# Gate one-hots in pairs of tokens, a U tile in every second gate step, and gate sums evicted with four tokens innermost

## The chip, the cores and the metric

The kernel runs on one core of a Trainium2 chip. The metric is the device time of one execution in microseconds (us). Before the change the median of 3 runs is 2675.46 us, from 2675.15 to 2679.0. The engines of the core are TensorE (matmuls, PE in the profile; its weight loads are PEld), VectorE (DVE), ScalarE (ACT), GpSimd (POOL) and SyncE (SP), whose queue issues most of the DMA transfers.

## The reference, cut to what matters

The program is two transformer blocks over 512 tokens of width 1024. The change lies in the PEER layer at the end of the first block. For every token, 8 heads choose 16 experts each out of 128 x 128, by the best sums of two keys, and a softmax over the 16 gives the gates. An expert is one row of `expert_u` and one of `expert_v`:

```python
eidx = take_along_axis(cand_idx, pos)      # i * 128 + j, for 512 tokens x 8 heads x 16
g = softmax(best)
for each block of tokens:
    u = expert_u[ib]                       # ib, gb: eidx and g of the block
    a = gelu(einsum('thkd,td->thk', u, xb))
    w = gb * a
    out = einsum('thk,thkd->td', w, expert_v[ib])
```

## The kernel before

The first three blocks of 128 tokens (`TD` = 384 tokens) do not gather rows of experts. They multiply all 16384 experts: `u_tile` makes Gelu(U h) for 128 experts and 384 tokens, `weighted` multiplies that with the gate sums of these experts, and `add_rows` multiplies the product with 128 rows of `expert_v` and adds it up in PSUM. The fourth block gathers its rows by indirect DMA (lines 938 to 957), spread over the same main loop of 128 steps (lines 1018 to 1039).

Gate sums are what `peer_gates` makes from line 1191 on. For one token, the 128 choices (8 heads x 16) lie on the partitions. A one-hot matrix `oj` says which second key j each choice has, and `o1` and `o2` say which first key i, times the gate in two fp16 parts. Two matmuls of 128x128x128 (lines 1229 and 1230) give the sum of gates for each (j, i) of that token. There are 384 tokens, so 768 such matmuls. A one-hot of 128 is the product of a high digit of 8 and a low digit of 16 (`onehot`, line 1219, on VectorE), and the digits themselves are compared with a ramp `rt` for 96 tokens at a time (`digit`, line 1202). The work goes in 48 steps of 8 tokens: three one-hots, two PSUM tiles `g_gp` of four tokens each, and two evictions by ScalarE (line 1232) to `g_sg`. Four steps fill a `g_sg` of 32 tokens, which goes to DRAM (`b_gd`, 2 MB, line 1235). The main loop reads it back as `b_g`, four experts' rows of keys at a time (line 965), and needs all 12 parts for its first step.

In DRAM and in `g_sg` the order is key i, then token. In the one-hots four tokens lie innermost: `[groups of 4 tokens, 128 keys, 4 tokens]`, so the columns of one token are 4 elements apart. The one-hot tiles have two buffers each, `g_gp` has four and `g_sg` two.

A U tile needs 512 KB of U by the SP queue, a split into a high and a low part (`w_hi` on ScalarE, `w_lo` on VectorE, lines 71 and 72), 24 matmuls of 128x384 (lines 76 to 78, `b_ups`) and a Gelu on ScalarE (line 915). U tiles do not depend on the gates, so they are strewn over `peer_gates` to fill TensorE: 28 calls stand ahead of the gate steps, 16 in them (every third step) and 2 after them (line 920). The activated tiles 0 to 9 lie in a part of `x` that is free for that time (`NX` = 10), the others in a pool of `NAB` = 36, and `b_ups` has two PSUM banks. A place of the pool is free again when `weighted` (line 969) has read it, and from step 10 on the main loop calls `u_tile` once in each step. The order on each engine is made by a scheduler that keeps the program's order as a priority, and lets an instruction pass another that is not ready.

Of the kernel before, what the change touches and what calls it, by code (L numbers as in the profile page):

```python
# [13 lines left out]
FP16 = mybir.dt.float16  # L14
I32 = mybir.dt.int32
U32 = mybir.dt.uint32
AF = mybir.ActivationFunctionType
OP = mybir.AluOpType
# [829 lines left out]
GS = 32768.0  # L848
# [4 lines left out]
GT = 32  # L853
OG = 8
DG = 3
# [27 lines left out]
def phase_b(K):  # L883
    nc, tc, d = K.nc, K.tc, K.d
    V, S, PE = nc.vector, nc.scalar, nc.tensor
    with ExitStack() as st:
# [31 lines left out]
        with ExitStack() as s1:  # L918
            peer_gates(K, s1, P, hT, small, gd, eg, gg3, u_tile)
# [132 lines left out]
def peer_gates(K, st, P, hT, small, gd, eg, gg3, u_tile):  # L1052
    nc, tc, d = K.nc, K.tc, K.d
    V, S, PE = nc.vector, nc.scalar, nc.tensor
    tk = st.enter_context(tc.tile_pool(name="g_tk", bufs=1))
    tT = tk.tile([128, 6, TD], FP16, name="g_tT")
    rt = tk.tile([128, 16, 16], FP16, name="g_rt")
    with ExitStack() as s0:
# [4 lines left out]
        with ExitStack() as s1:  # L1063
# [18 lines left out]
            for hp in range(16):  # L1082
                w, ps = began.pop(0)
# [25 lines left out]
        for b in range(NB):  # L1109
# [3 lines left out]
            for i in range(5):  # L1113
                n = LENS[i]
# [15 lines left out]
        n = NB * 128  # L1130
# [60 lines left out]
    with ExitStack() as s2:  # L1191
        ohp = s2.enter_context(tc.tile_pool(name="g_ohp", bufs=2))
        stg = s2.enter_context(tc.tile_pool(name="g_stg", bufs=2))
        gps = s2.enter_context(tc.tile_pool(name="g_gps", bufs=4, space=PSUM))
        dg = s2.enter_context(tc.tile_pool(name="g_dg", bufs=1))
        G4 = DG * GT // 4
        for c in range(TD // GT):
            if c % DG == 0:
                ts = slice(c * GT, (c + DG) * GT)
                token = lambda w: tT[:, w, ts].rearrange("p (g t) -> p g t", t=4)[:, :, None, :]  # L1200

                def digit(w, n):

                    t = dg.tile([128, G4, n, 4], FP16, name=f"g_d{w}")
                    V.tensor_tensor(t[:], token(w).to_broadcast(t[:].shape),
                                    rt[:, None, 0:n, 0:4].to_broadcast(t[:].shape), op=OP.is_equal)
                    return t[:]

                ih, jh, il, jl = digit(0, 8), digit(1, 8), digit(2, 16), digit(3, 16)
                ih0, ih1 = [dg.tile([128, G4, 8, 4], FP16, name=f"g_d{w}")[:] for w in (4, 5)]  # L1210
                for w, t in ((4, ih0), (5, ih1)):
                    V.tensor_tensor(t, ih, token(w).to_broadcast(t.shape), op=OP.mult)
            sg = stg.tile([128, 128, GT], F32, name="g_sg")
            for t8 in range(GT // OG):
                g0 = ((c % DG) * GT + t8 * OG) // 4
                gs = slice(g0, g0 + OG // 4)
                shape = [128, OG // 4, 8, 16, 4]

                def onehot(hi, lo, name):
                    t = ohp.tile([128, OG // 4, 128, 4], FP16, name=name)  # L1220
                    V.tensor_tensor(t[:].rearrange("p g (a b) t -> p g a b t", a=8), hi[:, gs, :, None].to_broadcast(shape),
                                    lo[:, gs, None].to_broadcast(shape), op=OP.mult)
                    return t

                oj, o1, o2 = onehot(jh, jl, "g_oj"), onehot(ih0, il, "g_o1"), onehot(ih1, il, "g_o2")
                for g in range(OG // 4):
                    ps = gps.tile([128, 4, 128], F32, name="g_gp")
                    for t in range(4):
                        PE.matmul(ps[:, t], oj[:, g, :, t], o1[:, g, :, t], start=True, stop=False)  # L1229
                        PE.matmul(ps[:, t], oj[:, g, :, t], o2[:, g, :, t], start=False, stop=True)  # L1230
                    tq = t8 * OG + 4 * g
                    S.activation(sg[:, :, tq:tq + 4].rearrange("p i t -> p t i"), ps[:], AF.Copy, scale=1.0 / GS)
                if (c * (GT // OG) + t8) % 3 == 0:
                    u_tile()
            nc.sync.dma_start(gd[:, :, c].rearrange("q p n -> p q n"), sg[:].rearrange("p (q i) t -> p q (i t)", i=4))

# [1147 lines left out]
```

## Time and profile before

| | |
|---|---|
| median of 3 runs | 2675.46 us |
| the profiled execution | 2677.02 us |
| its span, first to last instruction | 2675.2 us |
| TensorE busy (matmuls) | 2536.6 us, 95% |
| VectorE busy | 1781.9 us, 67% |
| ScalarE busy | 961.8 us, 36% |
| granted clock of TensorE, mean | 0.972 of full speed |
| gate steps, first to last matmul | 590.9 to 748.6 us |
| first matmul of the main loop | 767.25 us |

Shares of the span are means over stages that have different limits. The stage of the gate steps is some 160 us long, and the table says nothing about it alone; views of that stretch do.

### The profile page before, as it was taken

The numbers are of one execution on the slowest core, as the hardware profiler recorded it, in microseconds if no ns is written. First come the engines' busy times: TensorE is split into PE (matmuls) and PEld (weight loads), VectorE is DVE, ScalarE is ACT, GpSimd is POOL, SyncE is SP. The second block draws the span as 40 slices with busy tenths as digits, with TensorE's granted clock in tenths as the row PEclk, the third lists the DMA queues.
The fourth block names the chain that finished last, engine by engine and source line by source line (L and its number), as shares of the span: only waits on it lengthen the run. The fifth ranks groups of instructions, "written<-read, shape, count | busy, mean of one in ns | idle before, by whom it ended". The sixth has DMA issues, their size and how long they took to land.

```text
span 2675.2 us, 43755 instructions
## 1 busy us (share of the span) xinstructions
PE 2536.6 (95%) x17112; PEld 2121.5 (79%) x17112; DVE 1781.9 (67%) x3794; ACT 961.8 (36%) x1603; POOL 390.1 (15%) x269
## 2 busy tenths in 40 slices
PE   5999999899989999999999998999999989999985
PEld 4987888899978999999999887888797856555664
DVE  6654689987757777778878797676753673333334
ACT  3431432457743333333333335343532411111112
POOL 0000000000013455555545320000000000000001
PEclk8999899999999999999999999998999999999988
DMA  6226222236787899989988883222132489998896
GB/s 233 80 93 235 79 81 81 103 126 202 217 285 282 318 325 326 325 323 321 328 325 320 300 302 125 87 80 71 64 116 110 180 336 392 390 395 355 346 415 260
DMA packets 183485, 623.93 MB, mean 233 GB/s; under 512 B 15847, under 2 KB 66407, under 8 KB 156651
## 3 DMA queue, kind: packets, MB, share of 16 engines
q1 hardware_dynamic: 146410, 486.87, 48.6%
q0 software_dynamic: 36864, 134.23, 14.4%
q8 instruction: 135, 2.21, 0.3%
q14 instruction: 76, 0.61, 0.1%
HBM read 591.55 MB, written 29.49 MB: 232 GB/s over the span
## 4 chain that ended last, share of the span: by engine, by line
PE 82%; DVE 10%; DMA 5%; ACT 2%; issue 1%; SPq 0%; DVEq 0%; ACTq 0%
PE f_hp L1889 6%; PE b_acc L77 6%; PE b_acc L78 6%; PE b_acc L76 6%; PE b_ups L78 6%; PE b_ups L76 6%; PE b_ups L77 6%; PE p_acc L76 5%; PE p_acc L77 5%; PE p_acc L78 5%; PE f_yp L1931 3%; DMA f_w<-in_w 3%; PE f_xp L1788 2%; PE g_gp L1229 2%; PE g_gp L1230 2%; DVE w_lo L72 2%
## 5 line engine op out<-in xcount | busy, mean ns | idle before, releaser
L72 DVE TENSOR_TENSOR w_lo<-w_raw,w_hi 128x1024 fp32r<-128x1024 f32 x228 | 277.8, 1219 | 247.1 <-ACT w_hi L71 246.8
L71 ACT CAST w_hi<-w_raw 128x1024 fp32r<-128x1024 f32 x228 | 239.0, 1048 | 548.8 <-PE b_ups L77 281.1
L78 PE MATMUL b_ups<-hT,w_lo 128*128 128x384 f32 x1024 | 347.8, 340 | 6.7 <-DVE w_lo L72 6.5
L76 PE MATMUL b_ups<-hT,w_hi 128*128 128x384 f32 x1024 | 347.7, 340 | 1.3 <-ACT x_sb L915 1.0
L77 PE MATMUL b_ups<-hT,w_hi 128*128 128x384 f32 x1024 | 345.4, 337 | 0.0
L938 POOL DMA_INDIRECT x_sb<-in_u_rows,b_eg x128 | 193.4, 1511 | 991.2 <-ACT w_hi L71 767.8
L77 PE MATMUL b_acc<-b_vl,b_wh 128*128 128x512 f32 x756 | 296.8, 393 | 9.0 <-DVE b_vl L72 9.0
L76 PE MATMUL b_acc<-b_vh,b_wh 128*128 128x512 f32 x756 | 295.1, 391 | 1.7 <-ACT b_vh L71 1.7
L78 PE MATMUL b_acc<-b_vh,b_wl 128*128 128x512 f32 x756 | 296.1, 392 | 0.0
L77 PE MATMUL p_acc<-w_lo,hT 128*128 128x256 f32 x896 | 255.2, 285 | 9.5 <-DVE w_lo L72 9.5
L76 PE MATMUL p_acc<-w_hi,hT 128*128 128x256 f32 x896 | 257.7, 288 | 2.6 <-ACT hT L71 2.0
L78 PE MATMUL p_acc<-w_hi,hT 128*128 128x256 f32 x896 | 254.8, 285 | 0.2 <-DVE hT L72 0.2
L938 POOL DMA_INDIRECT x_sb<-in_v,b_eg x128 | 186.5, 1457 | 219.4 <-DVE b_accg L955 188.4
L78 PEld LDWEIGHTS b_ups<-hT,w_lo 128*128 128x128 f32 x1024 | 194.0, 189 | 8.6 <-DVE w_lo L72 8.6
L76 PEld LDWEIGHTS b_ups<-hT,w_hi 128*128 128x128 f32 x1024 | 194.0, 189 | 5.1 <-ACT x_sb L915 1.3
L77 PEld LDWEIGHTS b_ups<-hT,w_hi 128*128 128x128 f32 x1024 | 193.5, 189 | 3.2
L76 PEld LDWEIGHTS p_acc<-w_hi,hT 128*128 128x128 f32 x896 | 171.9, 192 | 18.6 <-issue 13.2
L77 PEld LDWEIGHTS p_acc<-w_lo,hT 128*128 128x128 f32 x896 | 172.5, 193 | 11.2 <-DVE w_lo L72 10.7
L71 ACT CAST b_wh<-b_wfull 128x384 fp32r<-128x384 f32 x128 | 65.6, 514 | 320.7 <-PE b_acc L77 317.7
L77 PEld LDWEIGHTS b_acc<-b_vl,b_wh 128*128 128x128 f32 x756 | 143.0, 189 | 37.8 <-DVE b_vl L72 10.7
L78 PEld LDWEIGHTS p_acc<-w_hi,hT 128*128 128x128 f32 x896 | 172.2, 192 | 1.0 <-DVE hT L72 0.4
L945 DVE SCALAR_TENSOR_TENSOR b_junkg<-x_sb,h2g 128x1024 bf16<-128x1024 f32 x128 | 156.3, 1221 | 24.9 <-DMA x_sb<-in_u_rows,b_eg 23.3
(659 smaller groups left out, 5083.6 us busy)
## 6 DMA issues: line engine op xcount, KB each, us to landing
f_w<-in_w SPq DMA_DIRECT2D x192, 1024.0 KB
w_raw<-in_u SPq DMA_DIRECT2D x128, 512.0 KB
b_vraw<-in_v SPq DMA_DIRECT2D x128, 512.0 KB
b_gd<-g_sg SPq DMA_DIRECT2D x12, 2048.0 KB
b_g<-b_gd SPq DMA_DIRECT2D x32, 768.0 KB
a_ar_t<-in_w_ada SPq DMA_DIRECT2D x32, 512.0 KB
w_raw<-in_w_tok SPq DMA_DIRECT2D x20, 512.0 KB
a_ar_t<-in_w_ada SPq DMA_DIRECT2D x8, 1024.0 KB
```

What stands on the lines that cost most here:

```text
L71: self.nc.scalar.copy(hi, src)
L72: self.nc.vector.tensor_tensor(lo, src, hi, op=OP.subtract)
L76: first = mm(ps, a[0], b[0], start=start, stop=False)
L77: mm(ps, a[0], b[1], start=False, stop=False)
L78: mm(ps, a[1], b[0], start=False, stop=stop)
L938: nc.gpsimd.indirect_dma_start(out=r, out_offset=None, in_=d[src], in_offset=bass.IndirectOffsetOnAxis(ap=eg[:, k:k + 1], axis=0))
L945: tc.keep_in_program_order(V.scalar_tensor_tensor(junk[:], r, 1.0, h2g[:], op0=OP.mult, op1=OP.mult, accum_out=ag[:, k:k + 1]))
L1229: PE.matmul(ps[:, t], oj[:, g, :, t], o1[:, g, :, t], start=True, stop=False)
L1230: PE.matmul(ps[:, t], oj[:, g, :, t], o2[:, g, :, t], start=False, stop=True)
L1788: PE.matmul(room[k // 4][:, k % 4, :n], hs[i][:, b, k * 128:(k + 1) * 128], sel[:, b, :n], start=k % 4 == 0 and i == 0 and b == 0, stop=i ...
L1889: last = PE.matmul(p, X[:, k], ts["w31", k // 2][:, c0:c0 + 512], start=k == 0, stop=k == 7, skip_group_check=True)
L1931: PE.matmul(p, gT[k], ts["w2", hf][:, k * 512:(k + 1) * 512], start=k == 0, stop=k == 3, skip_group_check=True)
```

## The change

One-hots and digits hold two tokens innermost instead of four, in twice as many groups, so that the columns of one token are 2 elements apart. The number of instructions and their sizes stay. A U tile is called for in every second of the 48 steps (24 calls) instead of every third (16). The eviction still reads the same PSUM tile and writes the same elements of `g_sg`, but goes through them key by key with the four tokens innermost, instead of token by token with the 128 keys innermost.

```diff
@@ -1193,31 +1193,31 @@
         stg = s2.enter_context(tc.tile_pool(name="g_stg", bufs=2))
         gps = s2.enter_context(tc.tile_pool(name="g_gps", bufs=4, space=PSUM))
         dg = s2.enter_context(tc.tile_pool(name="g_dg", bufs=1))
-        G4 = DG * GT // 4
+        GN = DG * GT // 2
         for c in range(TD // GT):
             if c % DG == 0:
                 ts = slice(c * GT, (c + DG) * GT)
-                token = lambda w: tT[:, w, ts].rearrange("p (g t) -> p g t", t=4)[:, :, None, :]
+                token = lambda w: tT[:, w, ts].rearrange("p (g t) -> p g t", t=2)[:, :, None, :]
 
                 def digit(w, n):
 
-                    t = dg.tile([128, G4, n, 4], FP16, name=f"g_d{w}")
+                    t = dg.tile([128, GN, n, 2], FP16, name=f"g_d{w}")
                     V.tensor_tensor(t[:], token(w).to_broadcast(t[:].shape),
-                                    rt[:, None, 0:n, 0:4].to_broadcast(t[:].shape), op=OP.is_equal)
+                                    rt[:, None, 0:n, 0:2].to_broadcast(t[:].shape), op=OP.is_equal)
                     return t[:]
 
                 ih, jh, il, jl = digit(0, 8), digit(1, 8), digit(2, 16), digit(3, 16)
-                ih0, ih1 = [dg.tile([128, G4, 8, 4], FP16, name=f"g_d{w}")[:] for w in (4, 5)]
+                ih0, ih1 = [dg.tile([128, GN, 8, 2], FP16, name=f"g_d{w}")[:] for w in (4, 5)]
                 for w, t in ((4, ih0), (5, ih1)):
                     V.tensor_tensor(t, ih, token(w).to_broadcast(t.shape), op=OP.mult)
             sg = stg.tile([128, 128, GT], F32, name="g_sg")
             for t8 in range(GT // OG):
-                g0 = ((c % DG) * GT + t8 * OG) // 4
-                gs = slice(g0, g0 + OG // 4)
-                shape = [128, OG // 4, 8, 16, 4]
+                g0 = ((c % DG) * GT + t8 * OG) // 2
+                gs = slice(g0, g0 + OG // 2)
+                shape = [128, OG // 2, 8, 16, 2]
 
                 def onehot(hi, lo, name):
-                    t = ohp.tile([128, OG // 4, 128, 4], FP16, name=name)
+                    t = ohp.tile([128, OG // 2, 128, 2], FP16, name=name)
                     V.tensor_tensor(t[:].rearrange("p g (a b) t -> p g a b t", a=8), hi[:, gs, :, None].to_broadcast(shape),
                                     lo[:, gs, None].to_broadcast(shape), op=OP.mult)
                     return t
@@ -1225,12 +1225,13 @@
                 oj, o1, o2 = onehot(jh, jl, "g_oj"), onehot(ih0, il, "g_o1"), onehot(ih1, il, "g_o2")
                 for g in range(OG // 4):
                     ps = gps.tile([128, 4, 128], F32, name="g_gp")
-                    for t in range(4):
-                        PE.matmul(ps[:, t], oj[:, g, :, t], o1[:, g, :, t], start=True, stop=False)
-                        PE.matmul(ps[:, t], oj[:, g, :, t], o2[:, g, :, t], start=False, stop=True)
+                    for q in range(4):
+                        j, t = divmod(4 * g + q, 2)
+                        PE.matmul(ps[:, q], oj[:, j, :, t], o1[:, j, :, t], start=True, stop=False)
+                        PE.matmul(ps[:, q], oj[:, j, :, t], o2[:, j, :, t], start=False, stop=True)
                     tq = t8 * OG + 4 * g
-                    S.activation(sg[:, :, tq:tq + 4].rearrange("p i t -> p t i"), ps[:], AF.Copy, scale=1.0 / GS)
-                if (c * (GT // OG) + t8) % 3 == 0:
+                    S.activation(sg[:, :, tq:tq + 4], ps[:].rearrange("p t i -> p i t"), AF.Copy, scale=1.0 / GS)
+                if t8 % 2 == 0:
                     u_tile()
             nc.sync.dma_start(gd[:, :, c].rearrange("q p n -> p q n"), sg[:].rearrange("p (q i) t -> p q (i t)", i=4))
 
```

## Rows read from the trace of the kernel before

**Rows 1.** Busy time by stretch: us, then PE, PEld, DVE, ACT, POOL, clock, DMA.
```profile
590.00:750.00 160.00, 160.00 (x1166) 151.38 (x1166) 115.31 (x172) 119.06 (x130) 0.00 (x0) 1.00 0.68 204
...
850.00:950.00 100.00, 100.00 (x510) 91.28 (x509) 80.04 (x117) 34.81 (x48) 48.95 (x33) 1.00 0.91 327
```

**Rows 2.** Groups by line, 590 to 751 us: busy, mean ns, idle before.
```profile
L1232 ACT ACTIVATE g_sg<-g_gp 128x512 f32<-128x512 f32 x96 | 97.2, 1163 | 22.2 <-PE g_gp L1230 13.4 <-issue 8.7
...
L1221 DVE TENSOR_TENSOR g_oj<-g_d,g_d 128x1024 f16<-128x1024 f16 x46 | 31.6, 687 | 29.5 <-PE g_gp L1230 29.5
...
L72 DVE TENSOR_TENSOR w_lo<-w_raw,w_hi 128x1024 fp32r<-128x1024 f32 x17 | 20.8, 1221 | 13.4 <-ACT w_hi L71 13.4
L71 ACT CAST w_hi<-w_raw 128x1024 fp32r<-128x1024 f32 x17 | 18.0, 1058 | 20.6 <-PE b_ups L77 20.6
L915 ACT ACTIVATE b_a<-b_ups 128x384 f32<-128x384 f32 x17 | 8.2, 483 | 0.0
L1205 DVE TENSOR_TENSOR g_d<-g_tT,g_rt 128x1536 f16<-128x1536 f16 (+1 forms) x11 | 8.1, 777 | 0.0
L1212 DVE TENSOR_TENSOR g_d<-g_d,g_tT 128x768 f16<-128x768 f16 x6 | 3.1, 550 | 0.0
```

**Rows 3.** Timeline of TensorE, a run of gate matmuls: start us, duration us.
```profile
646.75 0.30 PE L1230 MATMUL g_gp<-g_o,g_oj 128*128 128x128 f16 x1
...
650.30 0.29 PE L1230 MATMUL g_gp<-g_o,g_oj 128*128 128x128 f16 x1
```

**Rows 4.** Timeline of TensorE, U tiles 44 to 47.
```profile
749.09 0.34 PE L78 MATMUL b_ups<-hT,w_lo 128*128 128x384 f32 x1
...
765.21 0.34 PE L78 MATMUL b_ups<-hT,w_lo 128*128 128x384 f32 x1
```

**Rows 5.** The tile `g_gp` (first and last start), chain of waits, TensorE's timeline.
```profile
L1230 PE MATMUL g_gp<-g_o,g_oj x384: 284/297/303, 591.0 to 748.6; 128*128 128x128 f16 x192
...
750.26 9.31 DMA b_gd<-g_sg
759.71 4.95 DMA b_g<-b_gd
...
767.25 1.67 PE L76 MATMUL b_acc<-b_vh,b_wh 128*128 128x512 f32 x6 [1.71 <-ACT b_vh L71]
```

**Rows 6.** Gelus of U tiles (line 915) by stretch: ScalarE busy, clock, DMA.
```profile
590.00:750.00 160.00, 8.22 (x17) 1.00 0.68 204
...
760.00:797.00 37.00, 0.00 (x0) 0.91 0.84 320
```

**Rows 7.** Timeline of TensorE: fp16 matmuls whose operands are read without a step.
```profile
2185.01 3.75 PE L1788 MATMUL f_xp<-f_sel,f_hs 128*128 128x128 f16 x64
```

**Rows 8.** Timeline of TensorE: fp32r matmuls of 256 columns without a step.
```profile
2147.61 0.28 PE L78 MATMUL p_acc<-w_hi,x_oT 128*128 128x256 f32 x1
...
2150.44 0.28 PE L78 MATMUL p_acc<-w_hi,x_oT 128*128 128x256 f32 x1
```

**Rows 9.** Weight loads by form, whole span.
```profile
L1230 PEld LDWEIGHTS <-g_oj 128*128 128x128 f16 x384 | 45.0, 117 | 2.9 <-issue 2.3
...
L76 PEld LDWEIGHTS p_acc<-w_hi,x_oT 128*128 128x128 f32 x128 | 24.1, 188 | 0.2 <-issue 0.2
```

**Rows 10.** VectorE by form, whole span: without a re-read, and re-reading one word.
```profile
L525 DVE TENSOR_TENSOR a_ar_t<-a_ar_t 128x1024 f32<-128x1024 f32 x2 | 2.4, 1221 | 0.0
L844 DVE TENSOR_TENSOR a_ar_t<-a_ar_t,r_rs_y 128x1024 f32<-128x1024 f32 x2 | 2.4, 1220 | 0.0
```

**Rows 11.** ScalarE by form, whole span: a copy from PSUM.
```profile
L338 ACT COPY c_a_t<-p_tps 128x512 f32<-128x512 f32 x8 | 4.7, 582 | 7.0 <-PE p_tps L337 7.0
```

**Rows 12.** TensorE by stretch, start of the main loop: busy, granted clock, DMA.
```profile
779.90:783.70 3.80, 0.46 (x3) 0.83 0.78 315
783.70:789.00 5.30, 5.23 (x12) 0.50 0.81 300
789.00:794.00 5.00, 5.00 (x23) 0.97 0.91 363
```

## The prediction

> **What bounds the kernel now.** I read the busy time by stretch first, because the change touches one stretch only. From 590 to 750 us, where the gate sums are made, TensorE is busy for all 160.00 us at a granted clock of 1.00; VectorE is busy for 115 us and ScalarE for 119 [rows 1]. The table of groups says who waits: VectorE stands 29.5 us before `g_oj`, each time until TensorE has finished with an older one-hot, and ScalarE 13.4 us until a gate sum is done [rows 2]. So TensorE sets the pace of the gate steps. From 850 us on TensorE is also busy without a gap [rows 1], so what is won or lost here reaches the end of the program.
>
> Then I read the matmuls one by one. In a run of gate matmuls 30 starts take from 646.75 to 650.30, which is 118 ns each [rows 3]. A U tile is 24 matmuls at 173 ns (93 starts from 749.09 to 765.21), 4.16 us [rows 4]. The check of both: 768 x 0.118 + 20 x 4.16 = 173.8 us, and from the first gate matmul at 590.9 to the end of the last U tile at 765.4 there are 174.5 us.
>
> Last comes the chain of waits where the gate stage hands over to the main loop. The last gate matmul starts at 748.6; the last `g_sg` is issued to DRAM at 750.26 and lands 9.31 us later, `b_g` comes back in 4.95 us, and the first `b_acc` matmul starts at 767.25, 18.65 us after the last gate matmul [rows 5]. TensorE spends that time on U tiles 44 to 47, so almost none of it shows today. It could not do more: there are 10 + 36 places for activated U tiles and two PSUM banks. No Gelu runs from 760 to 797 us [rows 6], though U tiles are multiplied until 765: 46 and 47 wait in PSUM until `weighted(10)` frees a place.
>
> **The change part by part.** *The step of the one-hots.* A gate matmul reads its 128 columns 4 fp16 elements (8 bytes) apart, afterwards 2 elements (4 bytes). The nearest rows on both sides: 64 fp16 matmuls of the same size, read without a step, take 3.75 us, 59 ns each [rows 7], and 118 ns is today's price. Between them I go by a third row. fp32r matmuls of 256 columns also start every 118 ns (24 starts from 2147.61 to 2150.44) [rows 8]; they read 256 words of 4 bytes side by side, so as many 8-byte words, 128, as a gate matmul touches today. With a step of 4 bytes a gate matmul touches 64, and half of 118 is 59. The weight load could be the limit instead, since it has the same step; but it lasts 117 ns against 188 for the fp32r ones that start at the same pace [rows 9], so it looks shorter than what paces those. I take 60 ns, and keep 59 and 118.
>
> [...]
>
> *The number and form of the one-hots.* They stay 144 products of 128x1024 fp16 at 0.687 us [rows 2]. Their innermost run shrinks from two 4-byte words to one, and the high digit re-reads that one word 16 times. An fp32 product that re-reads one word 64 times takes 1220 ns, one with no re-read 1221 [rows 10], so I take no extra; the other end is one element per tick, 1.22 us. The digits (8.1 + 3.1 us in the window, for 36 steps: 0.62 us per two steps) read the ramp one word at a time with hops; today's hopping `g_sg` writes show that hops can cost, so up to twice that, 0.6 us a round, stays in the range.
>
> *The eviction.* ScalarE writes `g_sg` in single words 128 bytes apart and takes 1.163 us [rows 2]; a copy of the same size from PSUM with nothing apart takes 0.582 [rows 11]. After the change it writes runs of four words, but reads PSUM in hops of 512 bytes. I take a value near the middle; any up to today's is hidden, as the sum shows.
>
> *The U tiles.* 24 are asked for instead of 16, but 28 stand before the loop and only 48 can be multiplied before `weighted(10)`. So 20 (28 to 47) go into steps 0 to 39, and steps 40 to 47 and the hand-over have none. This is the cost of the change: 18.65 us of hand-over that were covered lie bare.
>
> **The sum.** Two steps and one U tile cost TensorE 32 x 0.060 + 4.16 = 6.08 us, VectorE 6 x 0.687 + 1.22 + 0.62 = 5.96, ScalarE 4 x (0.58 to 1.16) + 1.05 + 0.48 = 3.9 to 6.2. TensorE still ends last, by a hair. 20 rounds take 121.6 us: 590.9 + 121.6 = 712.5. In the last 8 steps VectorE ends last: 8 x 2.06, plus the two splits for U tiles 48 and 49 (2.4), less two steps that it is ahead by its two buffers (4.1), plus the last 16 matmuls (1.0): 15.8. For three nearly equal engines with two buffers I add 2: the last gate matmul is at about 730, the first `b_acc` at 749, against 767.25: 18.3 us won.
>
> The bare wait costs clock too. [...] That is 2.6 us, which I charge once. The main loop itself I leave as it is: the same U tiles come as their places come free, and the order can cost a few us. 18.3 - 2.6 = 15.7. The profiled execution took 2677.0 us (span 2675.2), so 2661.3 like for like; the median of the three runs shown is 1.6 below it, hence **2660**.
>
> **The rivals.**
>
> *The pace stays at 118 ns* (slower). Weights may limit it, or 4 bytes may be no better than 8. The bunched U tiles then only bring the bare hand-over: 20 x (32 x 0.118 + 4.16) = 158.7, 8 x 1.89 = 15.1, so the last gate matmul is at 764.7 and the first `b_acc` at 783.4, 16.1 later, plus 2.6: 2694. It decides from 84 ns on: 640 matmuls x p = 54 us is what the gain can pay for. For it: pace and weight-load time are the same number today. Against it: [rows 7, 8]. [...]
>
> *The one-hots lose their rate.* At 1.22 us each VectorE needs 20 x 9.16 + 25, and the time is 2731; the change loses from 0.82 us a one-hot on. For it: no fp16 row here re-reads single words. Against it: [rows 10]. [...]
>
> *ScalarE becomes the bound.* 96 evictions must stay under 1.25 us. If reading in hops cost as much again as writing in hops does (0.58 on top of 1.163), the time would be 2722.
>
> *More is won.* If TensorE's queue keeps some U tiles back for the hand-over, VectorE alone ends the stage near 724 and no clock is lost: about 2650.
>
> **How the numbers follow.** My forecast 0.63 (its own range 2648 to 2669), more won 0.05, no difference through losses between the three engines 0.06, pace unchanged 0.17, one-hots or evictions slower 0.09. What a measurement of this kernel can tell from no change is 0.2%, 5.4 us. Faster 0.68, same 0.06, slower 0.26. The range 2647 to 2696 holds the forecast, no change and the unchanged pace, and leaves out the slow one-hots and evictions and the tail of the best case.
>
> **What would show it.** Gate matmuls 59 to 65 ns apart; one-hots at 0.69 us; evictions between 0.58 and 1.16; 20 U tiles' matmuls before the last gate matmul, which starts near 730; then TensorE idle for some 18 us, and a granted clock of about 0.5 after it. The prediction is wrong if gate matmuls still start 118 ns apart, if `g_oj` takes 0.8 us or more, or if TensorE is busy in the hand-over.

## The result, and the profile after

The changed kernel takes 2658.22 us (median of 4 runs, 2654.75 to 2660.13) where the kernel before, run beside it, takes 2676.64: a ratio of 0.9933, 95% interval 0.9918 to 0.9947. The forecast was 2660. The profiled execution took 2657.85 us, with a span of 2656.1. The lines of `peer_gates` from the second matmul on stand one further down than before (matmuls 1230 and 1231, eviction 1233).

TensorE's timeline of the changed kernel, a run of gate matmuls (start, duration, instruction), answers to [rows 3]:

```profile
599.80 0.22 PE L1230 MATMUL g_gp<-g_o,g_oj 128*128 128x128 f16 x1
...
601.12 0.22 PE L1231 MATMUL g_gp<-g_o,g_oj 128*128 128x128 f16 x1
```

These are 24 starts; the 23 steps between them take 1.32 us, 57 ns each, where there were 118. The groups by line from 590 to 740 us answer to [rows 2] (busy us, mean ns, idle before them):

```profile
L1233 ACT ACTIVATE g_sg<-g_gp 128x512 f32<-128x512 f32 x96 | 50.2, 601 | 16.8 <-PE g_gp L1231 8.2 <-issue 6.7 <-DMA b_gd<-g_sg 1.6
...
L1221 DVE TENSOR_TENSOR g_oj<-g_d,g_d 128x1024 f16<-128x1024 f16 x46 | 31.7, 688 | 0.3 <-PE g_gp L1231 0.3
...
L72 DVE TENSOR_TENSOR w_lo<-w_raw,w_hi 128x1024 fp32r<-128x1024 f32 x21 | 25.8, 1227 | 22.1 <-ACT w_hi L71 19.3 <-PE g_gp L1231 2.9
L71 ACT CAST w_hi<-w_raw 128x1024 fp32r<-128x1024 f32 x20 | 21.0, 1048 | 53.7 <-PE b_ups L77 53.7
L1205 DVE TENSOR_TENSOR g_d<-g_tT,g_rt 128x1536 f16<-128x1536 f16 (+1 forms) x11 | 14.5, 1370 | 0.0
```

The one-hots keep their time (688 ns) and no longer wait for TensorE: 0.3 us in place of 29.5. The eviction has halved, 601 ns. The digits have got dearer, 1370 ns in place of 777. VectorE's idle time now stands before `w_lo`.

The hand-over, answering to [rows 5], in the chain of waits and in TensorE's timeline:

```profile
736.10 10.01 DMA b_gd<-g_sg
...
746.18 4.32 DMA b_g<-b_gd
```

```profile
753.20 1.65 PE L76 MATMUL b_acc<-b_vh,b_wh 128*128 128x512 f32 x3 [17.84 <-ACT b_vh L71]
```

The last gate matmul starts at 735.1 in the view of the tile `g_gp` (748.6 before), and TensorE then stands for 17.84 us, where it stood for 1.71. The first matmul of the main loop comes 14.05 us earlier than before. Busy time by stretch of TensorE (us, busy, matmuls, granted clock, DMA) shows what the wait costs beside itself, and how the main loop starts:

```profile
753.20:755.00 1.80, 1.69 (x4) 0.50 1.04 424
755.00:760.00 5.00, 5.00 (x14) 0.58 0.91 292
760.00:765.00 5.00, 5.00 (x24) 1.00 0.93 351
...
770.00:800.00 30.00, 29.85 (x146) 1.00 0.59 202
800.00:850.00 50.00, 50.00 (x250) 1.00 0.74 255
```

After the idle time the granted clock is 0.50 and 0.58: 14 matmuls go into 5 us where 24 go into the next 5, so about 2.1 us are lost. From 770 to 850 us there is no gap. The same view of the kernel before does have gaps:

```profile
770.00:800.00 30.00, 24.91 (x97) 0.89 0.83 310
800.00:850.00 50.00, 46.12 (x208) 0.97 0.68 247
```

So the 19.1 us between the spans are 14.05 at the first matmul of the main loop and about 5 more in what follows it, up to 850 us (from there on TensorE has no gap in either kernel). That second part is in no term of the prediction.

### The profile page after: what moved, and what is told of

Read it like the earlier page. It is cut to its first block, busy times and chain, and to the rows that moved or that the text cites. A ratio compares the mean times of both kernels' runs of the same rounds, so it can differ in the third digit from the quotient of the medians.

```text
span 2656.1 us, 43750 instructions
## 1 busy us (share of the span) xinstructions
PE 2495.8 (94%) x17112; PEld 2079.8 (78%) x17112; DVE 1789.4 (67%) x3794; ACT 915.6 (34%) x1603; POOL 396.9 (15%) x269
## 3 DMA queue, kind: packets, MB, share of 16 engines
q0 software_dynamic: 36864, 134.23, 14.5%
## 4 chain that ended last, share of the span: by engine, by line
PE 79%; DVE 12%; DMA 3%; issue 3%; ACT 2%; POOL 0%; SPq 0%; DVEq 0%; ACTq 0%; POOLq 0%
PE f_hp L1890 6%; PE b_ups L76 6%; PE b_acc L77 6%; PE b_ups L78 6%; PE b_ups L77 6%; PE b_acc L78 5%; PE p_acc L76 5%; PE b_acc L76 5%; PE p_acc L77 5%; PE p_acc L78 5%; PE f_yp L1932 3%; PE f_xp L1789 2%; DVE w_lo L72 2%; PE f_hp L1876 2%; PE g_q L77 1%
## 5 line engine op out<-in xcount | busy, mean ns | idle before, releaser
L76 PEld LDWEIGHTS b_acc<-b_vh,b_wh 128*128 128x128 f32 x756 | 142.5, 189 | 45.1 <-ACT b_vh L71 18.0
L1890 PE MATMUL f_hp<-f_w,f_X 128*64 128x512 f32 (+1 forms) x640 | 171.4, 596 | 0.4 <-DVE f_X L1843 0.4
L955 DVE SCALAR_TENSOR_TENSOR b_accg<-x_sb,b_ag,b_accg 128x1024 f32<-128x1024 f32 x127 | 162.8, 1282 | 12.4 <-DMA x_sb<-in_v,b_eg 10.9
```

What stands on the lines that cost most here:

```text
L76: first = mm(ps, a[0], b[0], start=start, stop=False)
L955: tc.keep_in_program_order(V.scalar_tensor_tensor(accg[:], r, ag[:, k:k + 1], accg[:], op0=OP.mult, op1=OP.add))
L1890: last = PE.matmul(p, X[:, k], ts["w31", k // 2][:, c0:c0 + 512], start=k == 0, stop=k == 7, skip_group_check=True)
```

## Experiments

All times are medians beside runs of the kernel before on the same chip; ratios are to these, with 95% intervals. Between the sets of runs the median of the kernel before moves by 2 us, so a difference of 2 or 3 us between kernels of different sets is not shown. The first four kernels take the change apart.

| kernel | us | ratio | last gate matmul | first `b_acc` |
|---|---|---|---|---|
| before | 2675.7 to 2677.7 | 1 | 748.6 | 767.3 |
| changed | 2658.22 | 0.9933 (0.9918 to 0.9947) | 735.1 | 753.2 |
| pairs alone | 2650.25 | 0.9890 (0.9869 to 0.9911) | 718.8 | 740.6 |
| eviction alone | 2675.63 | 0.9998 (0.9985 to 1.0012) | 748.6 | 767.0 |
| U tiles alone | 2688.75 | 1.0032 (1.0019 to 1.0045) | 766.3 | 783.9 |
| pairs and eviction | 2650.96 | 0.9890 (0.9868 to 0.9911) | 720.0 | 741.1 |

**Pairs alone.** The kernel before with the new one-hots and digits, and with these two lines as they were:

```diff
-                    S.activation(sg[:, :, tq:tq + 4], ps[:].rearrange("p t i -> p i t"), AF.Copy, scale=1.0 / GS)
-                if t8 % 2 == 0:
+                    S.activation(sg[:, :, tq:tq + 4].rearrange("p i t -> p t i"), ps[:], AF.Copy, scale=1.0 / GS)
+                if (c * (GT // OG) + t8) % 3 == 0:
```

> The kernel before with digits and one-hots in pairs alone: a U tile in every third step and the eviction as before. My theory (the step of the one-hots alone makes the gain): gate matmuls start 57 to 60 ns apart, evictions stay at 1.16 us, VectorE sets the pace. Its work in the 48 steps is 144 x 0.689 + 16 x 1.22 + 26.5 of digits = 145 us, 136 of it after the first gate matmul; ScalarE needs 96 x 1.163 + 16 x 1.53 = 136, nearly as much. Last gate matmul at 728 to 734, U tiles 44 to 47 cover the hand-over, first b_acc at 746 to 752, and the main loop goes as before: 2656 to 2662. Rival A (the U tiles must be bunched too, to win): 2665 or more. Rival B (the pace is set by the weights' or the eviction's order): matmuls stay at 118 ns, 2677.

It gains 27 us, more than the whole change, and ends 6 us below the expected range; both rivals fall. The last gate matmul is at 718.8, 9 us before the earliest that was expected. The expectation priced a one-hot at its mean duration of 0.689 us, and that was too much: VectorE's timeline of the changed kernel shows one-hots that follow each other 0.60 us apart.

```profile
725.20 0.69 DVE L1221 TENSOR_TENSOR g_oj<-g_d,g_d 128x1024 f16<-128x1024 f16 x1
725.80 1.29 DVE L1221 TENSOR_TENSOR g_o<-g_d,g_d 128x1024 f16<-128x1024 f16 x2
727.02 0.69 DVE L1221 TENSOR_TENSOR g_oj<-g_d,g_d 128x1024 f16<-128x1024 f16 x1
```

Three one-hots take 1.82 us from start to start, where three durations are 2.06. Over 144 one-hots that makes about 12 us.

**Eviction alone.** The first of the two lines above the other way round, on the kernel before.

> The kernel before with the eviction's new order alone. My theory: 0.60 us in place of 1.16 us each, ScalarE 119 down to 65 us in the gate steps, but TensorE sets their pace: no change of the time, 2674 to 2680. Rival (the eviction holds PSUM tiles that TensorE waits for, or delays the handover): TensorE is busy without a gap already, so at most the last eviction of the stage, 0.6 us. Rival 2 (ScalarE free sooner brings other work forward and moves the main loop): some us either way.

The eviction falls to 599 ns, ScalarE's wait for TensorE rises from 13.4 to 50.0 us, and the time stays. ScalarE was hidden, as the first theory says. With pairs it is hidden too: 2650.25 against 2650.96.

**U tiles alone.** Only `% 3` becomes `t8 % 2 == 0`.

> The kernel before with a U tile in every second step alone. My theory: 20 rounds of 32 x 0.118 + 4.16 us and 8 steps of 1.89 put the last gate matmul at 764.7 (748.6 before), the handover has no U tiles left (TensorE idle some 18 us), first b_acc at 783.4. With the main loop as before and 2.6 us of clock: 2694. If the 5.6 us that the changed kernel won at the start of the main loop come from the six more calls of U tiles that stand ahead of it: 2686 to 2690. Rival (the bunched U tiles help by themselves): 2677 or less.

It is 11 us slower by the medians, 9 by the ratio. The last gate matmul is at 766.3 (764.7 expected), the first `b_acc` at 783.9, 16.6 later than before, and TensorE stands 17.3 us at the hand-over. Some 5 us of the loss come back afterwards, which is the second figure of the expectation.

**Pairs and eviction.** The changed kernel with a U tile in every third step.

> The changed kernel with a U tile in every third step, as before (pairs and the new eviction stay). My theory: VectorE sets the pace of the stage, 4 splits fewer fall into it (4.9 us), so the last gate matmul is at 728 to 732 in place of 735.1; U tiles 44 to 47 run in the handover, and TensorE waits 2 us or less there in place of 17.8; first b_acc at 746 to 750. If the U tiles are only moved, the main loop starts with as many done as in the changed kernel, so the idle time was no loss of its own: 2654 to 2659, that is like the changed kernel (2658). Rival (the bare handover is a loss of some 16 us that the U tiles in every second step cause): 2645 or less. Rival 2 (the six calls more ahead of the main loop are worth 5 us there): 2659 to 2664.

7.3 us faster than the changed kernel, between the theory and the first rival. The gate steps end 15 us sooner (at 720.0, where 728 to 732 were expected): four U tiles (16.6 us of TensorE) have left them and run in the hand-over, where TensorE still waits for 4.2 us. From the last gate matmul to the first `b_acc` it is 21.1 us in place of 18.1, so 12 of the 15 us reach the main loop. That has its gaps again: 8.4 us of waits for `b_vl`.

**The digits.** On the changed kernel, and then on the last one, a copy of the ramp in which the two equal elements of each value lie side by side:

```diff
+    r2 = tk.tile([128, 16, 2], FP16, name="g_r2")
...
+        S.copy(r2[:], rtf[:, :, 0:2])
...
-                                    rt[:, None, 0:n, 0:2].to_broadcast(t[:].shape), op=OP.is_equal)
+                                    r2[:, None, 0:n].to_broadcast(t[:].shape), op=OP.is_equal)
```

> The changed kernel with a packed copy of the ramp for the digits (two elements of each of the 16 values side by side), so that their second operand is read without hops. My theory (the digits' hopping reads of single words are what I left out of the sum): L1205 goes from a mean of 1.37 us to 0.78, 6 us of VectorE in the stage; the last gate matmul comes 4 to 6 us sooner (729 to 731 in place of 735.1), the time is 2652 to 2655. Rival A (the ramp is not what costs; the re-read words of the tokens are): 1.37 us stay, 2658. Rival B (the digits get cheap, but what ends last is the wait of w_lo for w_hi in VectorE's queue, because a U tile comes every second step): 0.78 us, but 2656 to 2659.

2649.18 us, ratio 0.9906 (0.9887 to 0.9925): 9 us less than the changed kernel, more than expected. The wide digits by form, in the changed kernel, with the packed ramp, and in the kernel before:

```profile
L1205 DVE TENSOR_TENSOR g_d<-g_tT,g_rt 128x1536 f16<-128x1536 f16 x8 | 13.7, 1742 | 0.0
```

```profile
L1207 DVE TENSOR_TENSOR g_d<-g_tT,g_r 128x1536 f16<-128x1536 f16 x8 | 7.4, 950 | 0.0
```

```profile
L1205 DVE TENSOR_TENSOR g_d<-g_tT,g_rt 128x1536 f16<-128x1536 f16 x8 | 7.4, 956 | 0.0
```

Between the first two the output and the other operand are the same, so the 0.79 us is the hop from word to word in the ramp (32 bytes). The kernel before makes the same hop, but after every second word, and takes 956 ns, against 1742 with a hop at every single word. How this reaches TensorE is seen in the changed kernel's chain of waits, and in TensorE's timeline, where a matmul waits for a one-hot:

```profile
620.47 1.20 DVE g_o L1221 x2
621.68 4.15 DVE g_d L1205 x3
625.83 0.06 DVE g_d L1212
625.89 0.30 issue
626.19 0.58 DVE g_d L1212
626.77 0.60 DVE g_oj L1221
```

```profile
628.03 0.29 PE L1230 MATMUL g_gp<-g_o,g_oj 128*128 128x128 f16 x2 [2.22 <-DVE g_o L1221]
```

The digits of 96 tokens come in one piece, 5 us without a one-hot, and the two buffers of one-hots do not last that long. With the packed ramp the last gate matmul is at 725.2, 9.9 us sooner. That is more than the digits themselves have become cheaper (the group of line 1205 takes 14.5 us from 590 to 740, with the packed ramp 8.0 up to 735). Part of the rest is TensorE's clock. TensorE stands for 2.2 us at each of the three blocks of digits, and after two of them its granted clock falls; the stretch after the first, in the changed kernel and with the packed ramp:

```profile
628.00:634.00 6.00, 5.97 (x38) 0.72 0.99 290
```

```profile
628.00:634.00 6.00, 6.00 (x57) 1.00 1.01 269
```

From 707.5 to 713.5 it is 0.72 and 38 matmuls again; after the gap that ends at 668.6 it stays at 1.00. Rival B falls, though `w_lo` waits on (17.2 us): in a steady stretch that wait is only VectorE's slack under TensorE.

> The same packed ramp on the kernel with pairs, the new eviction and a U tile in every third step. My theory: there VectorE waits 10 us in 130 only, so the 6 us of digits show: last gate matmul at 713 to 716 in place of 719.9, first b_acc at 738 to 741, 2644 to 2648 in place of 2651. Rival (TensorE or the U tiles take over as the bound, or the main loop's start gives it back): 2649 to 2652.

2638.7 us, ratio 0.9865 (0.9846 to 0.9885), 12 us less than without the ramp, where 3 to 7 were expected; last gate matmul at 707.9 (713 to 716 expected). The granted clock in the gate steps is 1.00 here, where it is 0.96 without the ramp. From 588 to 708 us TensorE is now busy for 117.42 us of 120.00 and VectorE for 113.17, so both are nearly full.

**Which operand.** Two kernels made from the kernel before, each with one side in pairs and the other in fours (`TJ` is the number of tokens innermost in `oj`, `TI` in `o1` and `o2`; cut):

```diff
-                oj, o1, o2 = onehot(jh, jl, "g_oj"), onehot(ih0, il, "g_o1"), onehot(ih1, il, "g_o2")
+                oj, o1, o2 = onehot(jh, jl, "g_oj", TJ), onehot(ih0, il, "g_o1", TI), onehot(ih1, il, "g_o2", TI)
...
+                        j, t, i, s = *divmod(4 * g + q, TJ), *divmod(4 * g + q, TI)
```

> The kernel before with only oj (the weights) and its two digits in pairs; o1 and o2 (the moving operand) and their digits stay in fours; eviction and U tiles as before. Theory of the moving read (mine): weight loads fall from 117 to 99 ns, matmuls still start 118 ns apart, time 2675 to 2680. Rival (the weight load sets the pace): 57 to 70 ns, last gate matmul near 719, 2650 to 2656. Third way (either read alone is enough to hold the pace): 118 ns here and in the next kernel too.

> The kernel before with only o1 and o2 (the moving operand) and their digits in pairs; oj and its digits stay in fours. Theory of the moving read: matmuls 57 to 62 ns apart with weight loads still at 117 ns or less, last gate matmul near 717 (the digits jh and jl keep their cheap form), 2647 to 2652. Rival (the weight load sets the pace): 118 ns, 2677. Third way (each read alone holds it): 118 ns, 2677.

With only the weights in pairs the matmuls go on 116 ns apart (29 starts), 2674.33 us, ratio 0.9994 (0.9982 to 1.0006):

```profile
647.63 0.28 PE L1230 MATMUL g_gp<-g_o,g_oj 128*128 128x128 f16 x1
...
650.89 0.30 PE L1230 MATMUL g_gp<-g_o,g_oj 128*128 128x128 f16 x1
```

With only the moving operand in pairs:

```profile
650.43 0.22 PE L1230 MATMUL g_gp<-g_o,g_oj 128*128 128x128 f16 x1
...
651.79 0.23 PE L1231 MATMUL g_gp<-g_o,g_oj 128*128 128x128 f16 x1
```

```profile
L1230 PEld LDWEIGHTS <-g_oj 128*128 128x128 f16 x384 | 42.3, 115 | 9.9 <-DVE g_o L1221 6.6 <-issue 3.2
```

24 starts with 1.36 us from first to last, 59 ns each, while a weight load still lasts 115 ns: 2647.14 us, ratio 0.9885 (0.9867 to 0.9903). The pace hangs on the step of the moving operand; the weight load's record is twice as long as the pace and does not hold it. One expectation was wrong: weight loads in pairs alone are recorded at 113 to 116 ns on average, and do not fall to 99.

**One token innermost.** The kernel of 2638.7 us with `TI = TJ = 1` and a ramp of single elements.

> The kernel of the run before with the packed ramp and a U tile in every third step, but with one token in place of two innermost: the columns of one token lie side by side, and the high digit re-reads one fp16 element 16 times where a pair re-reads one 4-byte word. Theory (a re-read costs VectorE nothing, and a step of two elements costs TensorE nothing): one-hots 0.69 us, digits 0.77, matmuls 57 ns apart, 2637 to 2641 as with pairs (2638.7). Rival A (VectorE's rate hangs on whole 4-byte words, which is why pairs and not singles are used): one-hots 1.22 us, VectorE 144 x 0.53 = 76 us more, 2700 to 2716. Rival B (matmuls gain from no step at all): under 55 ns apart; no time follows, since VectorE sets the pace.

2716.85 us, ratio 1.0144 (1.0123 to 1.0166): rival A. Matmuls go 56 ns apart, so no step at all wins TensorE next to nothing over a step of two, but the one-hots have lost their rate:

```profile
L1223 DVE TENSOR_TENSOR g_oj<-g_d,g_d 128x1024 f16<-128x1024 f16 x48 | 58.5, 1219 | 0.6 <-PE g_gp L1233 0.6
```

The last gate matmul is at 787.4, 79.5 us after that with pairs (144 x 0.53 is 76). A one-hot takes 0.685 us with pairs and 1.219 where the high digit is one element re-read.

**The lead.** The changed kernel calls 52 U tiles ahead of the main loop, the kernel before 46. On the kernel before, and on that of 2638.7 us:

```diff
-        while len(acts) < NAB + NX:
+        while len(acts) < NAB + NX + 6:
```

> The kernel before with nothing changed in the gate steps, but 8 in place of 2 U tiles called after them: six calls stand ahead of the main loop, as in the changed kernel, and every later U tile is called six steps sooner. Theory (the lead is what makes the main loop's start 5 to 8 us shorter with the U tiles in every second step): gate steps as before (last matmul 748.6), first b_acc at 767, then TensorE waits 2 us or less for b_vl in place of 9.0: 2668 to 2673. Rival (that gain belongs to the bare handover, during which weights and rows are fetched ahead): 2675 to 2679.

> Pairs, the new eviction, the packed ramp, a U tile in every third step (2638.7) and six calls more ahead of the main loop. Theory of the lead: U tiles 44 to 47 still cover the handover, and the 6.9 us that TensorE waits for b_vl at the main loop's start go: 2631 to 2635. Rival (the gain belongs to the bare handover): 2637 to 2641.

The first takes 2671.37 us, ratio 0.9978 (0.9962 to 0.9994), as expected; the second 2635.68, ratio 0.9845 (0.9825 to 0.9865), just above the 2631 to 2635 expected. VectorE's waits from 766 to 850 us, and TensorE's from 735 to 900, in the kernel before (us in total, times, longest):

```profile
DVE b_junkg L945 <- DMA x_sb<-in_u_rows,b_eg: 16.6, 4, 6.6
```

```profile
PE b_acc L77 <- DVE b_vl L72: 9.0, 3, 3.9
```

With the lead on the kernel before no such wait is left on either engine, and TensorE is busy for 79.79 us of 770 to 850, where it was busy for 71.03:

```profile
770.00:800.00 30.00, 29.89 (x137) 1.00 0.79 299
800.00:850.00 50.00, 49.90 (x248) 1.00 0.70 242
```

The first of the gathered rows' products (line 945) comes at 815.8 in place of 774.8. The hand-over is still covered (3.0 us of waiting, 1.7 before), and the main loop starts without gaps all the same, so the gain belongs to the lead and not to the bare wait. With the packed ramp and a U tile in every third step 3.0 us are left of it by the medians, with intervals that overlap, so there the gain is not shown; the waits for `b_vl` (6.9 us) are gone, but the wait at the hand-over grows from 4.2 to 7.0 us, where it was expected to stay covered. Among the kernels here this one has the lowest median, 1.55% below the kernel before.

## Why the prediction was right, and what cancelled in it

*The step of the one-hots.* Right, and for the reason given: the moving read, 57 ns in place of the 60 taken. The rival that the pace stays at 118 is excluded by the run with the moving operand alone. That words of 8 bytes are what counts was the author's estimate from [rows 7, 8]; no run shows it, and with no step, where half as many are touched as with pairs, the pace is 56 ns.

*One-hots and eviction.* Right: 0.688 us, and 0.601 near the lower bound of 0.582. That a re-read of one word costs nothing held for the 4-byte word of a pair, at 0.688 us. For one fp16 element it did not: the run with one token innermost shows the case of 1.219 us that the second rival feared. The "one element per tick" of the other end is the pace of the fp32 products in [rows 10]: 1024 elements in 1.22 us, 1.19 ns each.

*The rounds of two steps and one U tile.* The forecast was 6.08 us with TensorE ending last, with 20 U tiles in the steps. Both are so: between the first and the last gate matmul the trace has 480 matmuls of `b_ups`, 24 for each of 20 U tiles, and where no digits are made a U tile starts every 6.07 us (589.00, 595.07, 601.14, 607.22). With 57 ns a matmul the terms give 5.98, so the 60 ns taken hid 0.1 us that is in no term. VectorE's 5.96 was priced too high, by durations that overlap; it has slack and waits for `w_hi`. The prediction calls every eviction up to 1.163 us hidden, but its own sum gives ScalarE 6.2 us a round for that, more than 6.08; at the 0.60 us measured this did no harm.

What failed is the digits' extra cost, taken at 0 with up to 0.6 us a round kept in the range: with the ramp packed the stage ends 9.9 us sooner (735.1 against 725.2), 0.5 a round. The form was wrong too, for it is no cost per round: the digits come in blocks that starve TensorE, and the granted clock falls to 0.72 after two of them. Two rounds without digits take 12.15 us; the two rounds around each block take 16.3, 14.7 and 16.3 us, 10.6 us more in all, and 12.8 each time with the packed ramp. So the 20 rounds take 132.2 us (588.1 to 720.3) in place of 121.6. Two smaller errors work the other way. The gate steps begin at 588.1, 2.8 us sooner than before, which is in no term, and the last eight steps take 14.8 us, where 15.8 and 2 more for losses were taken. Together that puts the last gate matmul at 735.1 in place of 730.

*The hand-over.* Right: the first `b_acc` comes 18.1 us after the last gate matmul (18.65 taken), TensorE stands 17.84 us, and the clock after it is 0.50 to 0.58; 2.1 us are lost to it from 755 to 760 where 2.6 were charged in all. The 2.6 follow from [rows 12]: 12 matmuls take 5.23 us at a granted clock of 0.50, where 23 go into 5.00 at 0.97. That the bunched U tiles are the cost of the change was right in kind, and measured: with a U tile in every third step the kernel is 7.3 us faster. Its gate steps end 15 us sooner, but 3 us of that go into the longer hand-over and about 6 into the main loop, which has lost its lead of six U tiles and waits again.

*The main loop, left as it is.* Wrong: with the clock's 2.6 us the sum loses time after the first `b_acc`, and about 5 us were won there. The six calls ahead of it were named among the U tiles (24 in place of 16), but not what they do to the order on VectorE.

So the total of 2660 against 2658 owes something to luck, to two errors of opposite sign: 18.3 us were forecast at the first `b_acc` and 14.05 won, and after it a loss of 2.6 was forecast and some 5 us won. Between the profiled executions that makes 15.7 forecast and 19.1 measured, and each error alone is larger than this difference. The size of the clock's term at the hand-over and the gain of the one-hots stand by the runs; the closeness of the total does not prove them.

What stays open is why the scheduler puts the gathered rows' products later on VectorE when U tiles are called sooner. That it does so, and that the waits go with it, is shown; the order itself was not varied alone.

## What to carry to other kernels

The layout of a tile has two readers with different wishes: here TensorE's matmuls started every 57 ns with the moving operand's columns 4 bytes apart and every 118 ns with 8, VectorE made a one-hot in 0.69 us with pairs and in 1.22 with single elements, and pairs of fp16 satisfy both. When a layout changes, every other operand that follows its shape (here a ramp of 16 values) has to be looked at, and a short burst on a hidden engine counts against the buffers ahead of it, not against its mean: here 5 us of digits let TensorE stand for 2.2 us, and after two of the three gaps the granted clock was 0.72. Fillers for TensorE are worth most where it would otherwise stand, so they should be kept for the hand-over and not be spent where the stage is already full: here a U tile in every third step was 7.3 us faster than one in every second.

## What the runs showed of the hardware that was not expected

- A weight load recorded at 115 ns does not hold matmuls that start every 59 ns.
- VectorE's recorded durations overlap: one-hots of 0.69 us follow each other at 0.60.
- Matmuls of 128 fp16 columns start every 57 ns with a step of two elements and every 56 ns with none, against 118 with a step of four.
- After two of three gaps of 2.2 us in its work TensorE's granted clock was 0.72 over the next 6 us, after the third 1.00.
- The same eviction takes 1.16 us when it writes single words 128 bytes apart and 0.60 when it writes four side by side, though it then reads PSUM in hops of 512 bytes.
